# Holding the three-block sums of a softmax on VectorE in program order

## The chip, the cores and the metric

The kernel runs on one core of one Trainium2 chip. The core has five engines with a queue each: TensorE (PE in the rows), VectorE (DVE), ScalarE (ACT), GpSimd (POOL) and SyncE (SP), which only issues transfers here. The metric is the device time of one execution in microseconds. Three runs of the kernel before took 3987.66, 3991.29 and 3997.23 us; the median is 3991.29 us.

## The reference, cut to what matters

A backbone of two layers over 2048 latent and 256 context tokens of width 1024, all in float32. Layer 0 is multi-head latent attention with 16 heads, layer 1 gated linear attention. The edit is in the attention of layer 0:

```python
def one_block(qi):
    s = jnp.einsum('bqhrd,bkhd->bhrqk', qi, k, preferred_element_type=F32) * scale
    p = jax.nn.softmax(s, axis=-1).astype(v.dtype)
    return jnp.einsum('bhrqk,bkhe->bqhre', p, v)
...
oc = attention_blocks(qc, kc, vc)
ox = attention_blocks(qx, jnp.concatenate([kc, kx], axis=1), jnp.concatenate([vc, vx], axis=1))
```

Context queries see the 256 context tokens; latent queries see all 2304.

## The kernel before, in words

The attention handles two heads at a time (8 pairs). Per pair there are five steps: one of 256 context queries against 2 blocks of 128 keys, and four of 512 latent queries against 18 blocks. A step and a block make an item: 592 items in all.

**Per item.** `scores` (line 626) issues ten matmuls into `st` (two buffers), for both heads of the pair; keys and queries are split in two terms each for precision. ScalarE takes the exponential (line 628) into a slot of `pe`, a ring of nine slots in SBUF. `values` (line 663) multiplies a slot with the value rows into `po`, which accumulates over a whole step.

**Groups.** Items go in groups of six (a context step makes a group of two). After the scores of the first item of the next group, `burst` issues the values of the whole group in one run, 24 matmuls of 512 columns, and then whatever hangs on a step's end: `finish` (line 678 to 683) for the step before, a piece of the next layer's modulation (`mods`, lines 72 to 100), the closing of a step's maxima, and `gated` (line 669), which multiplies `po` by a gate.

**The softmax's denominators.** They are sums of exponentials over the blocks, gathered in `acc` by GpSimd (line 643). Of the six blocks of a large group, GpSimd adds the last three itself, one by one. The first three are added up by VectorE first: `thirds` issues four TENSOR_REDUCE instructions (line 652), each of which sums three neighbouring slots for one head and 256 queries into `part` (one buffer), and GpSimd then adds `part` to `acc`. In the rest of this document these four instructions are "the sums". In the source they come after the values of their group.

**The maxima.** The softmax subtracts a maximum per query, found ahead of time, about a step and a half early: TensorE computes approximate products of later queries and keys into `pmx` (line 491, three buffers, two in use for a pair) and VectorE takes the row maximum of each (line 493, `mx`). A generator hands them out, one pair of heads per call, at a rate that spreads them over the items: two maxima per item, in some items four. When a step's maxima are done they are closed: `mc` (line 502) reduces them, TensorE transposes the result (line 505), VectorE negates it (`mr`, line 508) and SyncE puts it into the queries.

**What sets the order.** A scheduler places every instruction in its engine's queue, by dependences and by costs that it assumes; an engine then runs its queue in that order and waits at its head. Instructions handed to `tc.keep_in_program_order` are the exception: they stand in the order of the source relative to each other. In this stage the variable `pinned` turns that on for all of TensorE's matmuls (`pe_op`). VectorE's maxima and sums are placed by the scheduler.

Of the kernel before, what the change touches and what calls it, by code (L numbers as in the profile page):

```python
# [14 lines left out]
ALU = mybir.AluOpType  # L15
AX = mybir.AxisListType
# [106 lines left out]
def body(ctx, tc, I, out, stop=99, dbg=None):  # L123
    nc = tc.nc
# [83 lines left out]
    with pool("p1", 2) as sp, pool("ps1", 2, space=PSUM) as psp:  # L208
# [60 lines left out]
        for ci, (c0, n) in enumerate(CHUNKS):  # L269
# [12 lines left out]
            for (w0, m, what) in groups:  # L282
# [22 lines left out]
                elif isinstance(what, int):  # L305
                    nc.vector.tensor_copy(raw[:, what, :n], ps[:, :n])
                    j = 0 if what < 3 else 1
# [293 lines left out]
    with pool("p3", 2) as sp, pool("ps3", 2, space=PSUM) as psp:  # L601
# [30 lines left out]
        def slot(si, kt):  # L632
            pr, ci = steps[si]
            return (75 * pr + (3 + 18 * (ci - 1) if ci else 0) + kt) % RING

        def add(si, part):

            n = CHUNKS[steps[si][1]][1]
            st_ = live[si]
            st_["seen"].append(part)  # L640
            if len(st_["seen"]) > 1:
                a = st_["seen"][0] if len(st_["seen"]) == 2 else st_["acc"]
                nc.gpsimd.tensor_tensor(st_["acc"][:, :, :n], a[:, :, :n], part[:, :, :n], op=ALU.add)  # L643

        def thirds(si, kt):

            part = sp.tile([P, 2, 512], F32, name="part", bufs=1)
            s0 = slot(si, kt)
            for j in range(2):
                for c in (0, 256):  # L650
                    src = ring[:, s0:s0 + 3, j, c:c + 256].rearrange("p s c -> p c s")
                    nc.vector.tensor_reduce(part[:, j, c:c + 256], src, axis=AX.X, op=ALU.add)  # L652
            add(si, part)

        def values(si, kt, nk):
# [89 lines left out]
        def burst(i, end=False):  # L745

            nonlocal nv, nb
            group = items[nv:i]
            nv = i
            nb += 1  # L750
            cl = list(closes)
            closes.clear()
            for c in cl:
                next(c)
            for si, kt, nk in group:
                values(si, kt, nk)
            while done:
                finish(done.pop(0))
            if nb > 4 and nb % 3 == 0 and i < len(items) - 70:
                next(extra, None)  # L760
            for c in cl:
                next(c)
            for si, kt, nk in group:
                if nk > 2 and kt % 6 == 0:
                    thirds(si, kt)
            si, kt, nk = group[-1]
            if kt == nk - 1:
                gated(si)
                done.append(si)
            for c in cl:  # L770
                next(c, None)
# [774 lines left out]
```

## Time and profile before

| | |
|---|---|
| median of three runs | 3991.29 us (3987.66 to 3997.23) |
| the profiled execution | 3990.15 us |
| its span, first to last instruction | 3988.3 us |
| TensorE matmuls busy | 3658.7 us (92%) |
| VectorE busy | 2258.8 us (57%) |
| ScalarE busy | 1335.6 us (33%) |
| GpSimd busy | 1402.2 us (35%) |
| mean granted TensorE clock | 0.967 |

The attention stage lies between about 692 and 2608 us of the span. Busy time is the time in which an engine executes; an engine that waits at the head of its queue is idle, and the views name the instruction whose end released it. The granted clock is a share of TensorE's full speed: 1.00 is 2.4 GHz and 0.50 is 1.2 GHz.

### The profile page before, as it was taken

The numbers are of one execution on the slowest core, as the hardware profiler recorded it, in microseconds if no ns is written. First come the engines' busy times: TensorE is split into PE (matmuls) and PEld (weight loads), VectorE is DVE, ScalarE is ACT, GpSimd is POOL, SyncE is SP. The second block draws the span as 40 slices with busy tenths as digits, with TensorE's granted clock in tenths as the row PEclk, the third lists the DMA queues.
The fourth block names the chain that finished last, engine by engine and source line by source line (L and its number), as shares of the span: only waits on it lengthen the run. The fifth ranks groups of instructions, "written<-read, shape, count | busy, mean of one in ns | idle before, by whom it ended". The sixth has DMA issues, their size and how long they took to land.

```text
span 3988.3 us, 59297 instructions
## 1 busy us (share of the span) xinstructions
PE 3658.7 (92%) x24126; PEld 2721.2 (68%) x24126; DVE 2258.8 (57%) x3356; ACT 1335.6 (33%) x1951; POOL 1402.2 (35%) x867
## 2 busy tenths in 40 slices
PE   7999999888988888888888888999999999999799
PEld 5777876555555555555555555577899899999677
DVE  4433325555555655655656566446336777776863
ACT  2322221333333333333333333423224444444441
POOL 3121123455465554645556555555300100000000
PEclk9999999999999999999999999999999999999899
DMA  6211564211111111111111000057776566658432
GB/s 219 82 60 46 201 224 119 68 38 50 48 30 53 43 48 36 50 34 46 48 36 53 19 23 31 9 169 245 244 252 208 196 224 207 235 184 308 158 133 95
DMA packets 280921, 456.01 MB, mean 114 GB/s; under 512 B 23028, under 2 KB 179764, under 8 KB 268680
## 3 DMA queue, kind: packets, MB, share of 16 engines
q1 hardware_dynamic: 216312, 375.21, 28.5%
q10 hardware_dynamic: 64336, 77.02, 5.7%
q8 instruction: 189, 3.10, 0.3%
q14 instruction: 84, 0.69, 0.1%
HBM read 311.27 MB, written 140.71 MB: 113 GB/s over the span
## 4 chain that ended last, share of the span: by engine, by line
PE 64%; DVE 17%; DMA 7%; issue 6%; POOL 2%; ACT 2%; SPq 1%; ACTq 0%; POOLq 0%; DVEq 0%
PE po L663 13%; PE st L626 12%; DVE part L652 8%; PE pmx L491 7%; DVE mx L493 5%; PE pj L60 4%; PE pj L61 4%; PE pj L62 4%; PE pp L964 2%; PE pp L965 2%; PE pp L966 2%; PE py L61 1%; PE py L60 1%; PE py L62 1%; DMA wsg<-in_gla_w_in 1%
## 5 line engine op out<-in xcount | busy, mean ns | idle before, releaser
L493 DVE TENSOR_REDUCE mx<-pmx 128x1 f32<-128x512 f32 (+1 forms) x1312 | 764.3, 626 | 380.0 <-PE pmx L491 375.7
L628 ACT ACTIVATE pe<-st 128x1024 f32<-128x1024 f32 (+1 forms) x592 | 600.0, 1014 | 1034.7 <-PE st L626 983.3
L626 PE MATMUL st<-qs,kbs 64*128 64x512 f32 (+2 forms) x5920 | 897.6, 409 | 3.1 <-ACT pe L628 3.0
L491 PE MATMUL pmx<-kbs,qs 64*128 64x512 f32 (+1 forms) x2624 | 551.0, 414 | 213.5 <-DVE mx L493 203.3
L626 PEld LDWEIGHTS st<-qs,kbs 64*128 64x128 f32 (+1 forms) x5920 | 669.5, 198 | 110.1 <-ACT pe L628 7.8
L643 POOL TENSOR_TENSOR acc<-acc,pe 128x1024 f32<-128x1024 f32 x224 | 532.2, 2376 | 449.6 <-ACT pe L628 416.4
L491 PEld LDWEIGHTS pmx<-kbs,qs 64*128 64x128 f32 x2624 | 311.2, 197 | 401.9 <-DVE mx L493 301.0
L663 PE MATMUL po<-pe,vt 128*64 128x512 f32 (+1 forms) x2368 | 525.6, 592 | 6.4 <-DMA vt<-v_d 6.4
L652 DVE TENSOR_REDUCE part<-pe 128x256 f32<-128x768 f32 x384 | 380.4, 1029 | 34.5 <-ACT pe L628 34.3
L663 PEld LDWEIGHTS po<-pe,vt 128*64 128x64 f32 x2368 | 160.9, 137 | 320.6 <-issue 309.4
L964 PE MATMUL pp<-w,ht 128*128 128x256 f32 x1088 | 317.5, 292 | 0.0
L965 PE MATMUL pp<-w,ht 128*128 128x256 f32 x1088 | 305.4, 281 | 0.0
L966 PE MATMUL pp<-w,ht 128*128 128x256 f32 x1088 | 304.5, 280 | 0.0
L1313 POOL TENSOR_TENSOR orr<-oss,mhalf 128x4 f32<-128x4 f32 x16 | 17.1, 1067 | 659.1 <-DVE oss L1312 659.1
L643 POOL TENSOR_TENSOR acc<-acc,part 128x1024 f32<-128x1024 f32 x96 | 229.2, 2388 | 7.5
L964 PEld LDWEIGHTS pp<-w,ht 128*128 128x128 f32 x1088 | 205.1, 189 | 3.5
L965 PEld LDWEIGHTS pp<-w,ht 128*128 128x128 f32 x1088 | 205.4, 189 | 1.1
L966 PEld LDWEIGHTS pp<-w,ht 128*128 128x128 f32 x1088 | 205.1, 188 | 0.1
L964 PE MATMUL pp<-ht,w 128*128 128x256 f32 (+1 forms) x616 | 184.9, 300 | 10.4 <-ACT vge L1029 8.5
L965 PE MATMUL pp<-ht,w 128*128 128x256 f32 (+1 forms) x616 | 176.8, 287 | 0.0
L966 PE MATMUL pp<-ht,w 128*128 128x256 f32 (+1 forms) x616 | 176.2, 286 | 0.1
L119 POOL TENSOR_TENSOR rs_r<-rs_v,mhalf 128x1 f32<-128x1 f32 x52 | 29.2, 562 | 381.7 <-DVE rs_v L117 381.7
(369 smaller groups left out, 6204.5 us busy)
## 6 DMA issues: line engine op xcount, KB each, us to landing
ht<-hh_d SPq DMA_DIRECT2D x44, 1024.0 KB
ht<-hl_d SPq DMA_DIRECT2D x44, 1024.0 KB
xt<-in_x SPq DMA_DIRECT2D x32, 512.0 KB
mod_w<-in_ada_w SPq DMA_DIRECT2D x16, 1024.0 KB
v<-gv_d SPq DMA_DIRECT2D x32, 512.0 KB
wsg<-in_gla_w_in SPq DMA_DIRECT2D x66, 192.0 KB
v_d<-vs ACTq DMA_DIRECT2D x18, 512.0 KB
vt<-v_d SPq DMA_DIRECT2D x8, 1152.0 KB
```

Source lines behind the costliest of these rows:

```text
L60: nc.tensor.matmul(ps, ah, bh, start=(i == 0), stop=False)
L61: nc.tensor.matmul(ps, ah, bl, start=False, stop=False)
L491: pe_op(nc.tensor.matmul(ps[j][:, :w], qs[js, 0, i, t * P:t * P + P], kk[js, bs], start=(i == 0), stop=(i == 1)))
L493: nc.vector.reduce_max(mx[:, j * nq + t, b:b + 1], ps[j][:, :w], axis=AX.X)
L626: pe_op(nc.tensor.matmul(st[:, j, :n], a[js, ks], qs[js, s, r, :n], start=(i == 0), stop=(i == len(terms) - 1)))
L628: nc.scalar.activation(pe[:, :, :n], st[:, :, :n], AF.Exp, scale=SCALE)
L643: nc.gpsimd.tensor_tensor(st_["acc"][:, :, :n], a[:, :, :n], part[:, :, :n], op=ALU.add)
L652: nc.vector.tensor_reduce(part[:, j, c:c + 256], src, axis=AX.X, op=ALU.add)
L663: pe_op(nc.tensor.matmul(po[64 * j:64 * j + 64, :n], vt[:, kt, 64 * j:64 * j + 64], pe[:, j, :n], start=(kt == 0), stop=(kt == nk - 1)))
L964: nc.tensor.matmul(ps, ah, bh, start=(i == 0), stop=False)
L965: nc.tensor.matmul(ps, ah, bl, start=False, stop=False)
L966: nc.tensor.matmul(ps, al, bh, start=False, stop=(i == n - 1))
```

## The change

One call is wrapped. The four sums of `thirds` are handed to `tc.keep_in_program_order`, so that they stand in the source's order relative to the other instructions that are held so, which in this stage are TensorE's matmuls.

```diff
@@ -649,7 +649,7 @@
             for j in range(2):
                 for c in (0, 256):
                     src = ring[:, s0:s0 + 3, j, c:c + 256].rearrange("p s c -> p c s")
-                    nc.vector.tensor_reduce(part[:, j, c:c + 256], src, axis=AX.X, op=ALU.add)
+                    tc.keep_in_program_order(nc.vector.tensor_reduce(part[:, j, c:c + 256], src, axis=AX.X, op=ALU.add))
             add(si, part)
```

TensorE's and ScalarE's queues are the same in both kernels. On GpSimd a few additions of `part` change places with neighbouring loads of keys, and on SyncE a few loads trade places. VectorE's queue changes throughout the stage, in three ways.

On VectorE, in the group whose sums run from about 1479 us in the trace of before, an ordinary group that ends a step (`ob` is `gated`). Before:

```order
L493 TENSOR_REDUCE mx<-pmx 128x1 x6
L652 TENSOR_REDUCE part<-pe 128x256 x3
L493 TENSOR_REDUCE mx<-pmx 128x1 x2
L652 TENSOR_REDUCE part<-pe 128x256
L493 TENSOR_REDUCE mx<-pmx 128x1 x4
L669 TENSOR_TENSOR ob<-po,gt 128x512
```

And now:

```order
L493 TENSOR_REDUCE mx<-pmx 128x1 x12
L652 TENSOR_REDUCE part<-pe 128x256 x4
L669 TENSOR_TENSOR ob<-po,gt 128x512
```

The four sums have moved behind the last six of the group's twelve maxima, and stand ahead of `ob`, which waits for the values.

On VectorE, one group earlier (sums from 1457.9 us), a group in which a step's maxima close (`mc`). Before:

```order
L493 TENSOR_REDUCE mx<-pmx 128x1 x10
L652 TENSOR_REDUCE part<-pe 128x256
L502 TENSOR_REDUCE mc<-mx 128x8
L652 TENSOR_REDUCE part<-pe 128x256 x2
L493 TENSOR_REDUCE mx<-pmx 128x1 x2
L652 TENSOR_REDUCE part<-pe 128x256
L493 TENSOR_REDUCE mx<-pmx 128x1 x6
L508 TENSOR_SCALAR mr<-pmx 8x128
```

And now (the first row begins in this group):

```order
L493 TENSOR_REDUCE mx<-pmx 128x1 x6
L502 TENSOR_REDUCE mc<-mx 128x8
L652 TENSOR_REDUCE part<-pe 128x256 x3
L493 TENSOR_REDUCE mx<-pmx 128x1 x2
L652 TENSOR_REDUCE part<-pe 128x256
L493 TENSOR_REDUCE mx<-pmx 128x1 x6
L508 TENSOR_SCALAR mr<-pmx 8x128
```

The first sum has moved behind `mc`; the sums still stand ahead of the group's last eight maxima, with a pair between them.

On VectorE, the group from 1506.4 us on, which also closes maxima and whose burst holds a piece of the modulation (`mod_s`). Before:

```order
L652 TENSOR_REDUCE part<-pe 128x256
L502 TENSOR_REDUCE mc<-mx 128x8
L652 TENSOR_REDUCE part<-pe 128x256 x2
L493 TENSOR_REDUCE mx<-pmx 128x1 x2
L652 TENSOR_REDUCE part<-pe 128x256
L493 TENSOR_REDUCE mx<-pmx 128x1 x6
L508 TENSOR_SCALAR mr<-pmx 8x128
L79 TENSOR_TENSOR mod_s<-mod_s,mod_b 2x512
L493 TENSOR_REDUCE mx<-pmx 128x1 x6
```

And now:

```order
L502 TENSOR_REDUCE mc<-mx 128x8
L493 TENSOR_REDUCE mx<-pmx 128x1 x8
L508 TENSOR_SCALAR mr<-pmx 8x128
L79 TENSOR_TENSOR mod_s<-mod_s,mod_b 2x512
L652 TENSOR_REDUCE part<-pe 128x256 x4
L493 TENSOR_REDUCE mx<-pmx 128x1 x12
```

The four sums have moved behind the group's last maxima, and behind `mr` and `mod_s` too, which wait for matmuls that follow the values; the maxima of the next group stand behind them.

## Rows read from the trace of the kernel before

**Rows 1.** Stretches: us, busy us of PE, PEld, DVE, ACT, POOL; clock, DMA share, GB/s.

```profile
703.60:2548.90 1845.30, 1638.43 (x10757) 1008.48 (x10757) 1114.07 (x1743) 628.89 (x660) 1012.21 (x512) 0.96 0.13 40
2548.90:2600.90 52.00, 51.94 (x334) 27.13 (x333) 15.34 (x17) 24.82 (x25) 32.56 (x15) 1.00 0.02 6
```

**Rows 2.** Groups by line, 703.6 to 2548.9 us: busy us, mean ns, idle before, releasers.

```profile
L493 DVE TENSOR_REDUCE mx<-pmx 128x1 f32<-128x512 f32 (+1 forms) x1244 | 725.0, 626 | 337.4 <-PE pmx L491 333.2 <-PE st L626 0.4
...
L628 ACT ACTIVATE pe<-st 128x1024 f32<-128x1024 f32 (+1 forms) x565 | 573.2, 1015 | 1010.1 <-PE st L626 959.4 <-PE pmx L491 40.4 <-POOL acc L643 5.7
L491 PE MATMUL pmx<-kbs,qs 64*128 64x512 f32 (+1 forms) x2488 | 520.8, 413 | 203.8 <-DVE mx L493 201.4 <-DVE mr L508 0.3
L643 POOL TENSOR_TENSOR acc<-acc,pe 128x1024 f32<-128x1024 f32 x214 | 507.7, 2372 | 436.5 <-ACT pe L628 403.9 <-DVE mx L493 27.4
...
L652 DVE TENSOR_REDUCE part<-pe 128x256 f32<-128x768 f32 x368 | 364.8, 1029 | 8.9 <-ACT pe L628 8.7
```

**Rows 3.** Timeline around the values of one group: start us, length us, instruction.

```profile
1503.85 2.59 DVE L493 TENSOR_REDUCE mx<-pmx 128x1 f32<-128x512 f32 x4
...
1506.41 5.37 PE L663 MATMUL po<-pe,vt 128*64 128x512 f32 x24
...
1507.38 2.35 POOL L643 TENSOR_TENSOR acc<-acc,part 128x1024 f32<-128x1024 f32 x1
...
1513.34 1.29 DVE L493 TENSOR_REDUCE mx<-pmx 128x1 f32<-128x512 f32 x2 [6.90 <-PE pmx L491]
```

**Rows 4.** Timeline of the scores that follow; in brackets the idle time before.

```profile
1516.15 1.33 PE L626 MATMUL st<-qs,kbs 64*128 64x512 f32 x10
...
1517.30 1.04 DVE L652 TENSOR_REDUCE part<-pe 128x256 f32<-128x768 f32 x1 [0.20 <-ACT pe L628]
...
1517.78 1.34 PE L626 MATMUL st<-qs,kbs 64*128 64x512 f32 x10
...
1518.36 1.96 DVE L652 TENSOR_REDUCE part<-pe 128x256 f32<-128x768 f32 x2
...
1518.95 0.40 PE L491 MATMUL pmx<-kbs,qs 64*128 64x512 f32 x1
...
1520.98 0.50 PE L491 MATMUL pmx<-kbs,qs 64*128 64x512 f32 x2 [1.63 <-DVE mx L493]
...
1521.44 1.02 DVE L652 TENSOR_REDUCE part<-pe 128x256 f32<-128x768 f32 x1
1521.55 2.29 PE L626 MATMUL st<-qs,kbs 64*128 64x512 f32 x9
...
1525.06 0.73 PE L491 MATMUL pmx<-kbs,qs 64*128 64x512 f32 x3 [0.36 <-DVE mx L493]
```

**Rows 5.** Stretches of 2 us of the same scores, with the granted clock.

```profile
1518.00:1520.00 2.00, 1.35 (x11) 0.77 (x7) 2.00 (x4) 1.39 (x2) 1.32 (x1) 1.00 0.00 0
...
1522.00:1524.00 2.00, 2.00 (x12) 1.60 (x10) 1.66 (x3) 0.12 (x1) 1.50 (x1) 0.50 0.04 8
```

**Rows 6.** Timeline, the sums' gap in the first and the last group with maxima.

```profile
715.42 0.73 PE L491 MATMUL pmx<-kbs,qs 64*128 64x512 f32 x3 [1.43 <-DVE mx L493]
...
2544.67 0.50 PE L491 MATMUL pmx<-kbs,qs 64*128 64x256 f32 x3 [1.90 <-DVE mx L493]
```

**Rows 7.** Timeline, an item with four maxima and no sums near it.

```profile
726.62 0.50 PE L491 MATMUL pmx<-kbs,qs 64*128 64x256 f32 x3 [0.58 <-DVE mx L493]
```

**Rows 8.** Timeline after the values that end at 1532.3 us, around the modulation's line 79.

```profile
1534.25 0.94 PE L491 MATMUL pmx<-kbs,qs 64*128 64x256 f32 x4
...
1534.80 0.68 DVE L79 TENSOR_TENSOR mod_s<-mod_s,mod_b 2x512 f32<-2x512 f32 x1 [0.16 <-ACT mod_s L78]
...
1534.92 1.45 PE L626 MATMUL st<-qs,kbs 64*128 64x512 f32 x10
1535.41 0.73 DVE L493 TENSOR_REDUCE mx<-pmx 128x1 f32<-128x256 f32 x2
...
1536.08 0.75 PE L491 MATMUL pmx<-kbs,qs 64*128 64x512 f32 x4
```

## The prediction

> **What bounds the kernel now.** I read the page's busy shares and its list of costly lines first, and from there the attention stage, the only one that the edit touches. The view by stretches cuts it in two: from 703.6 to 2548.9 us scores, values and maxima run together, and TensorE is busy for 1638 of 1845 us at a granted clock of 0.96; from 2548.9 to 2600.9 us the same scores, values and sums run without any maxima, and TensorE is busy for 51.94 of 52 us at 1.00 [rows 1]. So TensorE bounds the stage, and what it loses, it loses to the maxima. The view by lines says so: ahead of line 491, the matmuls whose results the maxima read, TensorE sat idle for 201.4 us waiting for line 493, VectorE's maxima [rows 2]. No other releaser there reaches 7 us.
>
> VectorE is not short of time: it is busy for 1114 of 1845 us [rows 1]. The order of its work is the trouble. The timeline of one group of six key blocks shows it. During the values (24 matmuls, 5.37 us) VectorE has nothing to do: its last maximum ends at 1506.44 and the next starts at 1513.34, 6.90 us later [rows 3]. Then, in the middle of the scores, come the four sums, one, two and one, with a pair of maxima before the last. The two at 1518.36 hold VectorE for 1.96 us. TensorE has three buffers for the products that the maxima read; it fills the last free one at 1518.95 and cannot go on until VectorE has come back to a maximum, and stands still for 1.63 us, later for 0.36 us more [rows 4]. Right after that the granted clock falls from 1.00 to 0.50, from TensorE's 2.4 GHz level to its 1.2 GHz one, and nine score matmuls take 2.29 us where ten took 1.34 a moment before [rows 4, 5]. The first and the last of the groups with maxima show the same gap, 1.43 and 1.90 us [rows 6]; there are 92 such groups, and four more without maxima at the end.
>
> **What one group costs today.** Of the 201.4 us some are not the sums' doing: where one key block carries four maxima instead of two, TensorE runs out of buffers without any sum, 0.58 us in the row shown [rows 7]. Ahead of the sums I counted 40 gaps, about 17 us in all. That leaves 184 us over 92 groups, 2.0 us each. A mean clock of 0.96 means that 4% of 1845 us is lost, 74 us, or 0.8 us per group (rounding of the view: 65 to 83 us in all). In the stretch without maxima the clock stays at 1.00, so I put all of it down to the gaps. A group thus loses 2.8 us.
>
> One rule speaks against the second half of that. The Trainium skill (TensorE: Matmul & The Clock Gate, Part 1) warns that the number of matmuls run at the lower clock differs from run to run of the same kernel and should not be fitted. By it the clock term is no firm saving, and without it the sum below would come to about 3903 us. No trace here shows two runs side by side, but the three timed runs of the kernel lie within 9.6 us of each other, so I keep the term.
>
> **What the change moves.** TensorE's and ScalarE's orders stay as they are; on GpSimd the additions of the sums move by a few places; on SyncE a few loads trade places. The move is on VectorE, and I went through all 96 groups of its new order:
> - Held, 57 groups: the four sums stand behind the last maximum of the stretch and ahead of anything that needs the values' results.
> - Unmoved, 24 groups, those in which a step's maxima close (line 502): three sums, a pair of maxima and the fourth sum stand in the middle of the scores as before, at most one pair later.
> - Late, 11 groups: the sums stand behind an instruction that waits for TensorE's work after the values (line 79, 91, 93 or 669), so they start in the next stretch, ahead of its first maxima.
> - The last four groups have no maxima to delay.
>
> Held: the sums take 4 x 1.03 = 4.1 us [rows 2]. In the row shown VectorE came free 0.03 us after the values began, and had 6.9 us until the next maximum could start [rows 3]. So 4.1 us lie wholly beside TensorE's values, with over 1 us to spare before they end, and the gap of 2.0 us and its clock loss of 0.8 go. If that cover failed, the first maxima of the next stretch would wait; a free third buffer absorbs the first half microsecond. What is late next is TensorE itself: a key block takes it 1.63 us (from 1516.15 to 1517.78 [rows 4]), in which ScalarE needs 1.02 us for its exponential and VectorE 1.25 for a pair of maxima [rows 2]. GpSimd has four additions of 2.37 us, 9.5 us per group [rows 2], and the one that takes the sums' result now starts some 4 us into the values, where it started at 1.0 [rows 3]; it has until the next group's exponentials to do it. The exponentials of the next group that overwrite the summed slots come three key blocks after the values, later than the sums' end. I cost all that at nothing; if GpSimd were late in each held group by 0.5 us, it would be 28 us. Saving: 57 x 2.8 = 160 us.
>
> Four-maxima blocks: those that now come after the sums in a stretch lose their 0.58 us still, where today it is swallowed by the larger gap. About half of the groups have one, some of them already counted. I take 6 us back (0 to 15).
>
> Unmoved: 24 x 0. They keep their gaps. Shifted by one pair, a gap could be 0.5 us larger or smaller; plus or minus 12 us for the range.
>
> Late: no row shows four sums ahead of a stretch's first maxima, so I place them in the row that precedes them [rows 8]. Line 79 ends at 1535.48, sums would then run until 1539.6, and the first maximum would end at 1540.3. TensorE has issued its first pair of products at 1534.25, scores until 1536.4, and can start one of the two products of 1536.08 in the third buffer; from about 1536.5 to 1540.3 it stands still, 3.8 us. With the clock loss in the same proportion as above (0.8 per 2.0) that is 5.3 us, against the 2.8 us that the group loses today: 2.5 us worse. Below, if the gap were no longer than today's, nothing; above, with 5.3 us of gap and 2.1 of clock, 4.6 us worse. I take the value worked out from the row, 11 x 2.5 = 28 us, and keep 0 to 51.
>
> **Sum.** The profiled execution took 3990.15 us, 1.85 us more than its span of 3988.3, and the three runs have a median of 3991.29, so the profile is 1.1 us under it. 3988.3 - 160 + 6 + 28 = 3862 us of span, 3864 us of time: 3.2% faster. A difference of 0.2%, 8 us, is about what a measurement of this kernel can tell from none.
>
> **Rivals.**
> - The clock does not come back, or new small gaps stand where the sums end: only the idle is won, 57 x 2.0 = 114, less 6 and less 11 x 1.8 for the late groups' idle, 88 us: 3902 us. For it: I count 44 falls of the clock in 92 groups, all with much the same gap, so the gap alone does not decide it. Against it: 1.00 wherever TensorE has no gap [rows 1, 5].
> - The late groups cost nothing more than today and the unmoved ones also gain a little from a sum that slips under the values: 160 + 12 and no loss: about 3820 us. For it: the late sums' gap lies where the clock has just been full for the whole of the values. Against it: the place in the order leaves TensorE one buffer and VectorE 4.1 us of work.
> - Slower: the held sums do not start at the values' beginning but as late as the 11, because the single buffer that they write is still being read by GpSimd's addition, queued behind its loads of keys and queries. Then 68 groups pay 2.5 us each, +170 us: 4160 us. It decides from about 36 late groups on. Against it: that addition ended at most a few microseconds into the previous values, a whole group earlier, and GpSimd is busy for 1012 of 1845 us [rows 1].
> - The edit does nothing: the sums would have to wait in the new place for what they waited for in the old. The order shows them moved past 6 to 10 maxima in 57 groups, so this only holds if TensorE were limited by something else at once: 3990 us.
>
> **Chances.** Forecast, a saving between 100 and 150 us: 0.68. Only the idle, or a saving of 30 to 100 us: 0.14. More than 150 us: 0.11. Nothing: 0.03. Slower: 0.04. The range reaches over the forecast and most of its two neighbours, 3822 to 3910 us. Faster by over 0.2%: 0.93; within: 0.03; slower: 0.04.
>
> **What would show it.** Right: TensorE's idle ahead of line 491 falls from 201 us to some 115 (24 unmoved groups at 2.0, 11 late ones at 3.8, the four-maxima gaps at 23); the sums' rows stand beside line 663's; the clock of the stretch rises to 0.98 or so; the duration of one sum stays at 1.03 us. Wrong: sums starting after the values in held groups, GpSimd's additions or ScalarE's exponentials as new releasers ahead of lines 626 or 663, or a clock of 0.96 still.

## The result, and the profile after

| | before | after |
|---|---|---|
| median | 3989.74 us (4 runs, 3987.66 to 3997.23) | 3831.93 us (4 runs, 3829.67 to 3842.1) |
| ratio | | 0.9606, 95% interval 0.9585 to 0.9628 |
| span of the profiled execution | 3988.3 us | 3827.9 us |
| mean granted TensorE clock | 0.967 | 0.972 |

The change saves 158 us, 3.9%. The prediction said 126 us (3864, range 3822 to 3910).

The same two stretches of the stage in the profile of after (length, busy us of PE, PEld, DVE, ACT, POOL; clock; DMA share; GB/s):

```profile
702.40:2390.30 1687.90, 1572.67 (x10757) 987.94 (x10757) 1124.26 (x1741) 629.55 (x660) 1013.00 (x511) 0.97 0.14 44
2390.30:2442.40 52.10, 52.06 (x335) 27.30 (x335) 17.99 (x20) 24.86 (x26) 35.47 (x16) 1.00 0.02 6
```

Beside [rows 1]: the stretch with maxima is 157.4 us shorter, the one without them as long as it was. VectorE, ScalarE and GpSimd do the same work in it to within 1%; the busy time of TensorE's matmuls fell by 66 us although their number is the same, so some of them ran faster.

The groups by line, in the same stretch of after:

```profile
L493 DVE TENSOR_REDUCE mx<-pmx 128x1 f32<-128x512 f32 (+1 forms) x1244 | 727.2, 627 | 310.1 <-PE pmx L491 303.2 <-PE st L626 0.7
...
L628 ACT ACTIVATE pe<-st 128x1024 f32<-128x1024 f32 (+1 forms) x565 | 574.0, 1016 | 838.6 <-PE st L626 763.7 <-PE pmx L491 39.8 <-POOL acc L643 30.0
...
L491 PE MATMUL pmx<-kbs,qs 64*128 64x512 f32 (+1 forms) x2488 | 467.9, 396 | 99.8 <-DVE mx L493 96.3 <-DVE mr L508 2.4
L652 DVE TENSOR_REDUCE part<-pe 128x256 f32<-128x768 f32 x366 | 355.3, 1028 | 2.4 <-ACT pe L628 2.4
```

Beside [rows 2]: TensorE's wait for the maxima fell from 201.4 to 96.3 us. The sums take 1028 ns each as before. One other wait of TensorE has grown, from nothing to 12.2 us, at line 678, for GpSimd's additions; the part on the sizes comes back to it.

A held group in the timeline of after, the values and what follows them (start us, length us, instruction, idle before it):

```profile
1442.59 3.85 DVE L652 TENSOR_REDUCE part<-pe 128x256 f32<-128x768 f32 x4
1442.66 5.37 PE L663 MATMUL po<-pe,vt 128*64 128x512 f32 x24
...
1446.59 2.36 POOL L643 TENSOR_TENSOR acc<-acc,part 128x1024 f32<-128x1024 f32 x1 [1.05 <-DVE part L652]
...
1448.82 0.73 PE L491 MATMUL pmx<-kbs,qs 64*128 64x512 f32 x4
...
1449.58 1.29 DVE L493 TENSOR_REDUCE mx<-pmx 128x1 f32<-128x512 f32 x2 [3.14 <-PE pmx L491]
```

These are the values of [rows 3]. The four sums, back to back in 3.85 us, lie wholly beside them, and VectorE still idles for 3.14 us before the next maximum, where it idled for 6.90. The scores that follow run without a gap. The addition on GpSimd has moved from 1.0 to 3.9 us behind the start of the values.

A late group, the next one:

```profile
1467.94 0.68 DVE L79 TENSOR_TENSOR mod_s<-mod_s,mod_b 2x512 f32<-2x512 f32 x1 [0.17 <-ACT mod_s L78]
...
1468.55 3.84 DVE L652 TENSOR_REDUCE part<-pe 128x256 f32<-128x768 f32 x4
...
1469.22 0.40 PE L491 MATMUL pmx<-kbs,qs 64*128 64x512 f32 x1
...
1472.32 0.73 DVE L493 TENSOR_REDUCE mx<-pmx 128x1 f32<-128x256 f32 x2
...
1472.78 1.22 PE L491 MATMUL pmx<-kbs,qs 64*128 64x512 f32 x3 [3.17 <-DVE mx L493]
1473.38 2.76 PE L626 MATMUL st<-qs,kbs 64*128 64x512 f32 x10
```

The clock in its stretches of 2 us:

```profile
1470.00:1472.00 2.00, 0.00 (x0) 0.00 (x0) 2.00 (x3) 0.55 (x1) 0.00 (x0) 1.00 1.02 376
1472.00:1474.00 2.00, 1.22 (x6) 1.03 (x8) 1.44 (x4) 0.00 (x0) 1.46 (x1) 0.56 0.85 328
1474.00:1476.00 2.00, 2.00 (x14) 1.50 (x12) 0.91 (x2) 0.00 (x0) 0.91 (x1) 0.50 0.00 0
```

These are the instructions of [rows 8] with the sums behind line 79. TensorE stands still for 3.17 us, and ten scores then take 2.76 us at the lower clock, 1.2 GHz, where they take 1.33 at the full one [rows 4].

TensorE's order is the same in both kernels, so the stage can be cut in both at the first of each group's values, and the stretches compared one by one (I took the starts from the two timelines; changes in us). A stretch goes by the group whose values end it, because that group's sums stood in it before; a late group's sums now stand in the stretch behind its own:

| stretches | number | change | each |
|---|---|---|---|
| held, none of the below | 45 | -139.8 | -3.1 |
| first behind a context step | 7 | -5.0 | -0.7 |
| unmoved, not behind a late group | 20 | -16.5 | -0.8 |
| late, the group's own stretch | 10 | -31.2 | -3.1 |
| behind a late group | 11 | +30.0 | +2.7 |
| context steps and the end | 10 | +5.1 | |
| outside the stage | | -3.0 | |

The sum is -160.4 us, the difference of the spans (the last row is what that leaves). Six of the 57 held groups and four of the unmoved stand behind a late one, six more held and one late behind a context step.

The 5.1 us are one stretch, the one that the last context step's values end. VectorE splits output weights there (line 53). The wait of TensorE for the maxima behind them, in before:

```profile
2391.94 1.21 PE L491 MATMUL pmx<-kbs,qs 64*128 64x512 f32 x3 [3.13 <-DVE mx L493]
```

And in after, where the sums now stand ahead of these splits:

```profile
2240.15 3.85 DVE L652 TENSOR_REDUCE part<-pe 128x256 f32<-128x768 f32 x4
...
2243.91 5.13 DVE L53 TENSOR_TENSOR wo<-wso,wo 128x1024 fp32r<-128x1024 f32 x2
...
2250.30 1.22 PE L491 MATMUL pmx<-kbs,qs 64*128 64x512 f32 x3 [8.15 <-DVE mx L493]
```

The prediction had counted this group as held; its sums are beside the values only in part and push other work of VectorE back.

### The profile page after: what moved, and what is told of

It reads as the page before. It is cut to its first block, busy times and chain, and to the rows that moved or that the text cites. A ratio compares the mean times of both kernels' runs of the same rounds, so it can differ in the third digit from the quotient of the medians.

```text
span 3827.9 us, 59284 instructions
## 1 busy us (share of the span) xinstructions
PE 3588.8 (94%) x24126; PEld 2696.5 (70%) x24126; DVE 2272.0 (59%) x3356; ACT 1337.1 (35%) x1951; POOL 1406.1 (37%) x867
## 4 chain that ended last, share of the span: by engine, by line
PE 71%; DVE 9%; DMA 7%; issue 6%; POOL 4%; ACT 2%; SPq 1%; ACTq 0%; POOLq 0%; DVEq 0%
PE st L626 16%; PE po L663 12%; PE pmx L491 7%; PE pj L60 4%; PE pj L61 4%; PE pj L62 4%; PE pp L964 3%; DVE part L652 3%; PE pp L965 3%; PE pp L966 3%; DVE mx L493 2%; DMA wsg<-in_gla_w_in 1%; PE pg L1202 1%; PE py L964 1%; PE py L966 1%
## 5 line engine op out<-in xcount | busy, mean ns | idle before, releaser
L626 PE MATMUL st<-qs,kbs 64*128 64x512 f32 (+2 forms) x5920 | 858.0, 399 | 3.3 <-ACT pe L628 3.2
L626 PEld LDWEIGHTS st<-qs,kbs 64*128 64x128 f32 (+1 forms) x5920 | 638.5, 192 | 107.1 <-ACT pe L628 8.2
L491 PE MATMUL pmx<-kbs,qs 64*128 64x512 f32 (+1 forms) x2624 | 498.1, 398 | 110.0 <-DVE mx L493 98.2
```

What stands on the lines that cost most here:

```text
L491: pe_op(nc.tensor.matmul(ps[j][:, :w], qs[js, 0, i, t * P:t * P + P], kk[js, bs], start=(i == 0), stop=(i == 1)))
L626: pe_op(nc.tensor.matmul(st[:, j, :n], a[js, ks], qs[js, s, r, :n], start=(i == 0), stop=(i == len(terms) - 1)))
```

## The experiments

The theory: what counts is where the sums stand among VectorE's maxima; beside the values they are free, among the maxima they stop TensorE. TensorE's and ScalarE's queues are the same instruction for instruction in all kernels below. Ratios are to the kernel before.

**The sums right behind the values.** The edit, in `burst`:

```diff
             for si, kt, nk in group:
                 values(si, kt, nk)
+            for si, kt, nk in group:
+                if nk > 2 and kt % 6 == 0:
+                    thirds(si, kt)
             while done:
                 finish(done.pop(0))
...
-            for si, kt, nk in group:
-                if nk > 2 and kt % 6 == 0:
-                    thirds(si, kt)
```

> The changed kernel, with the held sums moved in the source from the end of a group's burst to right behind its values. On VectorE none of the sums stands behind lines 79, 91, 93 or 669 any more: of the 11 late groups about 8 become held and 3 unmoved, all else stays. Theory (the place of the sums among the maxima sets the time, and a late group pays a gap of its own): a late group costs about 4.5 us more than a held one, 8 x 4.5 plus 3 x 1.5, so some 40 us less than the changed kernel: 3790 us (3780 to 3805). Rival (late groups cost no more than held ones, and the whole gain came from the 57 held groups): 3830 us, within 8 us of the changed kernel.

Measured: 3782.95 us, ratio 0.9491 (0.9470 to 0.9513). Against 0.9606 that is 46 us of 3988; the late groups do cost that, and the rival falls. The group at line 53 stays as it was. Divided over the 8 that became held and the 3 that became unmoved, a late group costs 4 to 5 us more than a held one.

**All groups held.** The edit to the kernel before it:

```diff
-            for c in cl:
-                next(c)
             for si, kt, nk in group:
                 values(si, kt, nk)
             for si, kt, nk in group:
                 if nk > 2 and kt % 6 == 0:
                     thirds(si, kt)
+            for c in cl:
+                next(c)
```

> As the kernel before it, and the reduction that closes a step's maxima (line 502) moved in the source behind the sums. In VectorE's order 90 groups with maxima are then held and 2 unmoved; TensorE's and ScalarE's orders are unchanged. Theory (place): each of about 25 groups that were unmoved gains the 3.1 us that a held group gained, less the 16 us that such groups have gained already: some 60 us less than the kernel before it, 3725 us (3710 to 3745), and TensorE's idle ahead of line 491 falls to about 25 us, the gaps of the four-maxima blocks. Rival (GpSimd or ScalarE becomes the bound once all sums are late, or the closing of the maxima comes too late for the next step): 3790 us or more, with idle before lines 626 or 678 that ScalarE or GpSimd ends.

Measured: 3726.52 us, ratio 0.9348 (0.9321 to 0.9375), where the theory said 3725; in two groups of the 92 the sums stay in the middle of the scores. The waits of TensorE, by what ended them, in the whole span of this kernel (total, times, longest us):

```profile
PE pmx L491 <- DVE mx L493: 38.3, 52, 8.1
PE pmx L678 <- POOL acc L643: 18.6, 7, 4.8
```

Of the sums' gaps nearly nothing is left; the longest, 8.1 us, is the one behind line 53. A second wait has come up, at line 678, where the finished denominators are used.

**No sums at all.** The four sums are left out; GpSimd adds a constant tile in their place:

```diff
-            part = sp.tile([P, 2, 512], F32, name="part", bufs=1)
-            s0 = slot(si, kt)
-            for j in range(2):
...
+            part = fixed
             add(si, part)
```

> The changed kernel without the 384 sums: GpSimd adds a constant tile in place of each sum, so that its additions stay, and the denominators lack three blocks of six. TensorE's order is unchanged. This is what the sums cost in all. Theory (held sums are wholly hidden beside the values): the same time as with all groups held, within 15 us, about 3720 us; the sums then cost 270 us in the kernel before and 110 us in the changed one. Rival (held sums still cost something, by GpSimd's later addition or by running over the end of the values): 30 us or more below the kernel with all groups held.

Measured: 3709.29 us, ratio 0.9308 (0.9286 to 0.9331). So in the kernel before the sums cost 0.0692 x 3988 = 276 us; 384 sums of 1.03 us are 395 us of VectorE's time, so some were free even there. The change hides 157 us of the 276, and holding all groups 260. Of the 17 us that are left, 15 show in the waits of this kernel (line 675 is the 678 of the others):

```profile
PE pmx L491 <- DVE mx L493: 35.1, 51, 5.8
...
PE pmx L675 <- POOL acc L645: 6.5, 4, 4.8
```

The maxima's wait is 3 us shorter than with all groups held, most of it behind line 53 (the longest, 8.1 and 5.8 us), the denominators' 12 us.

**All groups late.** The sums are collected in a list and issued in the loop over items, held, ahead of the scores of the second item of the next group:

```diff
-            for si, kt, nk in group:
-                if nk > 2 and kt % 6 == 0:
-                    thirds(si, kt)
+            late.extend((si, kt) for si, kt, nk in group if nk > 2 and kt % 6 == 0)
...
+            while late:
+                thirds(*late.pop())
             scores(si, kt, nk)
```

> The changed kernel with the sums held one item later in the source, so that VectorE's order has all four of them behind the first pair of maxima of the next stretch and ahead of the second, in some 92 groups. TensorE's and ScalarE's orders are unchanged. The prediction's step for a late group (gap of 3.8 us and 1.5 us of clock, 2.5 us worse than in the middle of the scores): 92 x 2.5 us above the kernel before, 4220 us. By the changed kernel's trace (a late group costs 4.5 us, a held one saves 3.1, so 1.4 worse): 4120 us. Rival (a place is as good as another as long as it lies among the maxima): 3990 us.

Measured: 4136.24 us, ratio 1.0378 (1.0349 to 1.0407), 151 us above the kernel before, or 1.6 us per group of 92. Held in program order at the wrong place, the same sums cost more than where the scheduler had put them. The theory by the prediction's step had said 4220, the one by the changed kernel's trace 4120. One group in its timeline:

```profile
1507.78 3.86 DVE L652 TENSOR_REDUCE part<-pe 128x256 f32<-128x768 f32 x4
1509.17 0.28 PE L491 MATMUL pmx<-kbs,qs 64*128 64x256 f32 x1
...
1512.29 0.50 PE L491 MATMUL pmx<-kbs,qs 64*128 64x256 f32 x3 [2.84 <-DVE mx L493]
```

The gap is 2.84 us, and the mean clock of the whole run is 0.938. TensorE's waits in it:

```profile
PE pmx L491 <- DVE mx L493: 264.2, 126, 5.8
PE pmx L678 <- POOL acc L643: 34.7, 7, 12.7
```

The first was 203 us in 180 places before, the second 4.8 us. So the prediction's mechanism for a late group, one longer gap and more time at the lower clock, is seen here too. Its price of 2.5 us is not tested by this run: the sums stand behind a stretch's first pair of maxima here and ahead of it there, and some 30 of the 151 us are waits for denominators.

**Moved but not held.** All groups held, with the change itself undone:

```diff
-                    tc.keep_in_program_order(nc.vector.tensor_reduce(part[:, j, c:c + 256], src, axis=AX.X, op=ALU.add))
+                    nc.vector.tensor_reduce(part[:, j, c:c + 256], src, axis=AX.X, op=ALU.add)
```

> The kernel with all groups held, with the hold taken off the sums again: the source is the moved one (sums right behind the values, the closing of the maxima behind the sums), but the scheduler places the sums freely. On VectorE they stand in the middle of the scores in all 92 groups again. Theory (only the place in VectorE's order counts): the time of the kernel before, 3985 us within 10. Rival (the order of the source in itself, through the closing of the maxima or the loads, gives part of the gain): 3950 us or less.

Measured: 3983.59 us against 3983.23 of the kernel before on the same chip, ratio 0.9999 (0.9986 to 1.0012). The order of the source alone gives nothing; the place in the queue does.

**The additions held too.** All groups held, and on GpSimd in this stage the additions (line 643) and the splits of loaded keys in `load_k`:

```diff
-                nc.gpsimd.tensor_tensor(st_["acc"][:, :, :n], a[:, :, :n], part[:, :, :n], op=ALU.add)
+                (tc.keep_in_program_order if pinned else (lambda i_: i_))(nc.gpsimd.tensor_tensor(st_["acc"][:, :, :n], a[:, :, :n], part[:, :, :n], op=ALU.add))
...
-            if pr == 0 and ci < 2:
+            if pinned or (pr == 0 and ci < 2):
                 tc.keep_in_program_order(i_)
-            k.lo("p", dst[1], kf[:, 0, :n], dst[0])
+            pe_op(k.lo("p", dst[1], kf[:, 0, :n], dst[0]))
```

> The kernel with all groups held, and in the same stage GpSimd's additions to the denominators and its two splits of each loaded key block are held in program order too, so that the addition of the last sum of a pair of heads stands ahead of the next key block's split and not behind it. TensorE's, ScalarE's orders unchanged, VectorE's the same as with all groups held up to a few rows. Theory (what the held sums still cost is that line 678 waits 18.6 us in all, seven times, for an addition that GpSimd has queued behind key loads): these waits fall to about 6 us as without sums, 12 us less, 3714 us. Rival (the addition itself is late, because the sums end late, whatever stands ahead of it): 3726 us. A mishap that would show: keys split too late, TensorE then waits ahead of line 626 for GpSimd.

Measured: 3704.13 us, ratio 0.9299 (0.9283 to 0.9315), 20 us below the kernel with all groups held by the ratios, the fastest of all and level with the one without sums. The wait at line 678 fell as the theory said:

```profile
PE pmx L678 <- POOL acc L643: 6.8, 4, 4.8
```

The other 8 us or so are not the sums'. TensorE's first values in the kernel with all groups held had waited for the value rows, and that row has no counterpart here:

```profile
702.12 1.97 PE L663 MATMUL po<-pe,vt 128*64 128x256 f32 x8 [6.74 <-DMA vt<-v_d]
```

The key splits have left their places in the stage before. That this is what brought the value rows in time was not tried by itself.

## Why the prediction was right, and where its sizes were off

The time lies in the stated range, but the saving of 158 us lies above the forecast's own band of 100 to 150 us (chance 0.68), in the one that had 0.11. And there is luck in the range's holding: two costs that the prediction had at nothing, 12.2 us at line 678 and 5.1 us at line 53, took back part of what it had put too low. Without them the time would have been about 3815 us, below the range.

**The bound.** Right: TensorE lost its time to the maxima, and that loss was the sums' place. In after its idle time ahead of line 491 is 96.3 us, where the prediction said some 115; with all groups held it is 38.3 us, without sums 35.1. The clock of the stretch rose to 0.97, where it said 0.98 or so.

**A held group, 2.8 us.** Right in kind, too small: 3.1 us each in the 45 plain ones. TensorE's gaps there fell from 97.2 to 11.4 us and the time lost at the lower clock from 34.9 to 2.6 (half of each spell's busy time), together 2.6 us per group. The other half microsecond is a cost of a gap that no idle row shows. It goes by the number of gaps: the five of these stretches that lost no gap won 0.1 us less than idle time and clock together, the 15 that lost one won 0.4 us more, the 23 that lost two 0.7 us more; over all 67 gaps it is 0.33 us each.

Most of it can be seen in the rows. Where TensorE runs on, a block of fourteen matmuls takes 1.63 us [rows 4]; their records start in pairs, one for each head, so a pair follows the last after 0.23 us. But the record of a single matmul, whose end the profile models, lasts 0.40 us [rows 4], so the last one before a gap counts as busy for 0.17 us in which the next pair would have been under way. And behind a gap the second start comes late too. In the trace of before, at full clock:

```profile
1504.61 0.72 PE L491 MATMUL pmx<-kbs,qs 64*128 64x512 f32 x3 [0.93 <-DVE mx L493]
...
1504.95 1.54 PE L626 MATMUL st<-qs,kbs 64*128 64x512 f32 x10
```

Here 0.34 us pass instead of 0.23. I had counted idle time and clock, and not this. The 0.3 us between 2.8 and 3.1 are, over 57 groups, some 17 us of the 32 by which the forecast fell short.

**Unmoved groups, nothing.** Off by 16.5 us in 20 stretches. I had counted a group as unmoved when any maximum stood behind its sums. In some of them a step's maxima close late in the stretch, only one pair is left behind three sums, and most of the 4.1 us slid under the values all the same: three such stretches gained 5.5, 3.6 and 2.8 us, while most of the others changed by about 1 us or less either way. The clearest miss was in reading the order: the place that counts is how many maxima still stand behind the sums.

**Late groups, 2.5 us worse than today, 28 in all.** The direction was right, and the clock row falls as said. The gap was put too long: 3.8 us worked out, 3.17 in the row shown, and about 3.0 in the mean of the eleven, with one that had next to none. In the row the four sums took 3.84 us in place of 4.1, and the prediction gave one maximum the 0.7 us that two take in [rows 8] (0.73 us, x2). By the table the late groups' own stretches gained 31 us and the ones behind lost 30; since the stretches behind, had they not been late, would have gained some 18 us in their six held groups, the late groups came out about 18 us worse than before and not 28.

**What hides the cost elsewhere.** I had put GpSimd's later additions at nothing. They cost 12.2 us. TensorE's waits at line 678 by what ended them, of before and then of after (total, times, longest us):

```profile
PE pmx L678 <- POOL acc L643: 4.8, 1, 4.8
```

```profile
PE pmx L678 <- POOL acc L643: 17.0, 6, 4.8
```

The one of 4.8 us, at the end of the stage, is in both; the five new ones stand right behind a context step, where the values take 1.1 us instead of 5.4 and the queue holds the split of a key block ahead of the addition. The row of the first:

```profile
922.87 2.34 POOL L643 TENSOR_TENSOR acc<-acc,part 128x1024 f32<-128x1024 f32 x1
...
925.26 1.18 PE L678 MATMUL pmx<-acc,ones 128*64 128x512 f32 x4 [2.94 <-POOL acc L643]
```

Holding the additions, and with them the splits, took 12 us of it away, so it was the queue's order and not the sums' end.

**The clock term.** Of the 158 us some 33 came as clock (81 us lost in the stage before, 48 after, by the same reckoning on the two profiles). The forecast without it, 3903 us, was out by 71. The clock does differ between runs of one kernel: its mean lay between 0.963 and 0.970 in those of the kernel before. The Trainium skill (TensorE: Matmul & The Clock Gate, Part 1: The HAM clock gate) warns against fitting the number of matmuls at the lower clock, with figures for a kernel's start. The doubt that the prediction drew from it for the whole stage was not borne out: the runs of each kernel stayed within 24 us of each other, and the mean clock followed the gaps, from 0.938 with all groups late over 0.967 before to 0.983 with all held.

The prediction's argument that all groups had much the same gap, so that the gap alone did not decide the clock, was only half so. In 22 of the 92 stretches of before no gap reached 1.4 us, and the clock fell in two of these; it fell in 39 of the other 70.

**The rivals.** "Only the idle is won" fell with the clock's 33 us. "The late groups cost nothing more, the unmoved gain a little: about 3820 us" came closest in number, 12 us below the time measured, and is half right: the unmoved gained 16.5 us, but the late groups did cost, as the 46 us of the first experiment show. "Slower because the held sums start late" was not what happened. The kernel with all groups late, at 4136 us, shows that sums among the next maxima do slow it; it says nothing of that rival's cause, the buffer that GpSimd still reads, and that it comes near the rival's 4160 us is chance, since it has 92 late groups and not 68.

## What to carry to other kernels

Work of an engine that is busy for only 60% of the time can still stop the bounding engine, when it stands in the queue ahead of what gives that engine its buffers back; look for the stretch in which the bounding engine asks nothing of it, and put the work there. Read the order itself for every group, and count what still stands behind the moved instructions; a hold at the wrong place was worse than none (1.038 against 0.935 here). When a producer is moved later, look at its last consumer where the cover is shortest, here behind the short values of a context step.

## What the runs showed of the hardware

The granted clock fell to 0.50, the 1.2 GHz level, behind single short gaps of TensorE, but not behind each. By the trace of before, in the stretches with maxima: 26 of its 43 falls came in or right behind one of the 60 gaps between 1.4 and 2.05 us, 10 at one of the 13 longer ones, 7 at one of the 109 shorter ones.

A gap cost TensorE about 0.33 us more than its idle time and its time at the lower clock.

Sums on VectorE and additions on GpSimd do not slow each other here. In after, 125 sums ran wholly beside an addition and took 1030 ns in the mean, 129 ran beside none and took 1025; 38 of the full-width additions ran almost wholly beside sums and took 2376 ns, 209 beside none and took 2393.
